# Transposing the gated product of a feed-forward layer: TensorE against VectorE blocks and DMAs

## The chip, the core and the metric

One core of a Trainium2 chip runs the whole program. The metric is the device time of one execution in microseconds (us). The engines are TensorE (PE; its weight loads are shown apart as PEld), VectorE (DVE), ScalarE (ACT), GpSimd (POOL) and SyncE (SP). Each takes its own instructions strictly in its own order.

## What is computed

Two layers of a decoder trunk over 256 positions of width 1024, in float32. Each layer is a feed-forward half-step, a token mixer (gated convolution, sparse attention, cross-attention into 256 memory tokens) and a second feed-forward half-step. The change touches only the feed-forward half-steps, of which there are four:

```python
def swiglu(h, w_in, w_out):
    a, b = jnp.split(h @ w_in, 2, axis=-1)
    return (jax.nn.silu(a) * b) @ w_out

h = rms_norm(x, ffn1_norm_pre[l])
x = x + 0.5 * rms_norm(swiglu(h, ffn1_w_in[l], ffn1_w_out[l]), ffn1_norm_post[l])
```

`w_in` is 1024 x 5632 and `w_out` 2816 x 1024. The product `silu(a) * b` has a position in each row. The second product contracts over its 2816 columns, so TensorE needs it with those columns on the partitions: it has to be transposed.

## The kernel before

**Two streams.** The 256 positions are two streams of 128 rows, t = 0 and t = 1, written as Python generators (`stream`, L1150). A loop (L1159) takes one step of the one, then of the other; stream 0 may be up to three steps ahead. A step is one slice k of a product, six matmuls. A counter `now` counts the steps of both. `later(d, f)` calls f when `now` has gone on by d.

**Products in three matmuls.** Each operand is split in a rounded part and a rest (hi and lo), and `mm3` (L333) runs hi x hi, hi x lo, lo x hi into one PSUM bank (lines L334, L335, L336).

**Weights.** SP loads a unit of 128 x 1024 weights (512 KB) to one of 4 `raw` buffers. ACT writes `whi` (L276, with a gain, or L272), DVE writes `wlo` (L277 or L273), in one of 8 pairs of buffers. Both streams read the same unit, stream 0 first; when stream 1 has read it, its buffer is free. One row of ACT and one of DVE for each unit is thus the beat to which both engines work.

**A feed-forward layer** (`ffn`, L447) runs for j = 0 to 4 a product of 8 steps into two PSUM banks, `pa` and `pb`, then a half-width one (j = 5, 4 steps). After each, `gate` (L452) makes the gated product: ACT a tanh (`th`, L454), DVE two operations (L455 reads `pa`, L456 reads `pb`). When L456 is done the two banks are free. There are six banks of this kind (`psa`): each stream holds two, and two more are what the next product starts on.

**The transposition.** Three steps later `finish_gate` puts four TensorE transposes (L377, two for j = 5) into one of two other PSUM banks (`pst`); ACT copies the bank to `gT` hi (L368), DVE makes `gT` lo (L369). The output product (`output`, L431) then walks k = 0 to 21 over `gT[k // 4]`.

**What else bears on it.** GpSimd computes the small powers of the norms (L389 to L411) and issues a few small DMAs: `rest` (L186) and `stage` (L545 to L549), in layer 0 only, bring gains and constants that TensorE transposes (L188, L551). `begin_layer` starts, at k = 4 of the output product of the first feed-forward layer of each layer, the memory's keys and values, whose transposes (`m`) and products run beside that output product. SBUF tiles of 128 x 1024 come from one pool of 19 (`gtile`). All engines but SP are ordered by a list scheduler with costs of its own, so an instruction need not stand where the code puts it.

Of the kernel before, what the change touches and what calls it, by code (L numbers as in the profile page):

```python
# [21 lines left out]
F32 = mybir.dt.float32  # L22
F32R = mybir.dt.float32r
I32 = mybir.dt.int32
AF = mybir.ActivationFunctionType
OP = mybir.AluOpType
AX = mybir.AxisListType

P = 128
# [22 lines left out]
ABUFS = 6  # L52
LANES = 4
NORM_B, NORM_C = 1, 1
SILU = 3
CMP = 4
ATT_A, ATT_B, ATT_C, ATT_D = 1, 3, 2, 3

# [18 lines left out]


class Nothing:
    """Stands in for engines, pools and tiles while the order of the weight units is found."""  # L80

    def __getattr__(self, name):
        return self
# [11 lines left out]
def view(ap, off, dims):  # L95
    if isinstance(ap, Nothing):
        return ap
    return bass.AP(tensor=ap.tensor, offset=ap.offset + off, ap=[list(ap.ap[0])] + [list(d) for d in dims])


def f32(ap):
    return ap.bitcast(F32)


def trunk_kernel(tc: tile.TileContext, a, out: bass.AP):
    with ExitStack() as ctx:
        def pool(name, bufs, **kw):
            return ctx.enter_context(tc.tile_pool(name=name, bufs=bufs, **kw))

        pools = dict(  # L110
            consts=pool("consts", 1), rawp=pool("rawp", RAWBUFS), wp=pool("wp", WBUFS), gp=pool("gp", GBUFS),
            gbp=pool("gbp", GAINS), tp=pool("tp", TBUFS), sp_pool=pool("sp", 2),
            psa=pool("psa", ABUFS, space=bass.MemoryType.PSUM),
            pst=pool("pst", 8 - ABUFS, space=bass.MemoryType.PSUM))
        nothing = Nothing()
        plan = program(nothing, {k: nothing for k in pools}, nothing, nothing, None)
        with tc.manual_schedule(engines={mybir.EngineType.SP}):
            program(tc.nc, pools, a, out, plan)


def program(nc, pools, a, out, plan):
    dry = plan is None
    consts, rawp, wp, gp, gbp = (pools[k] for k in ("consts", "rawp", "wp", "gp", "gbp"))
    tp, sp_pool, psa, pst = (pools[k] for k in ("tp", "sp_pool", "psa", "pst"))

    class Small:
        @staticmethod
# [12 lines left out]
    def bank(name):  # L140
        return psa.tile([P, 512], F32, name=name, tag="a")

    def tbank():
        return pst.tile([P, 512], F32, name="pt", tag="t")

    def gtile(name, dt=F32):
        return gp.tile([P, 1024], dt, name=name, tag="g")

    def ttile(name, dt=F32):
        return tp.tile([P, 520], dt, name=name, tag="tmp")  # L150

# [1 line left out]
    x = [consts.tile([P, D], F32, name=f"x{t}") for t in range(2)]  # L153
    idle = ttile("idle", F32R)
    nc.vector.memset(f32(idle[:, :512]), 0.0)
# [22 lines left out]
    gT = consts.tile([P, 64], F32, name="gT")  # L178
# [9 lines left out]
        nc.tensor.transpose(pt[:, :48], rest[0:48, 0:P], ident[0:48, 0:48])  # L188
        nc.vector.tensor_copy(gT[:, 16:64], pt[:, :48])

# [1 line left out]
    now = [0]  # L192
    order, found, ready = [], {}, {}
    free = {"raw": RAWBUFS, "w": WBUFS, "g": GAINS}
# [128 lines left out]
    def later(delay, fn):  # L323
        serial[0] += 1
        deferred.append((now[0] + delay, serial[0], fn))
# [40 lines left out]
    def evac_split(hi, lo, ps, scale=None):  # L366
        if scale is None:
            nc.scalar.copy(hi, ps)  # L368
            nc.vector.tensor_sub(lo, ps, f32(hi))  # L369
        else:  # L370
            nc.scalar.activation(hi, ps, AF.Copy, scale=scale)
            nc.vector.scalar_tensor_tensor(lo, ps, scale, f32(hi), op0=OP.mult, op1=OP.subtract)

    def transpose4(src, c0, n=4):
        pt = tbank()
        for j in range(n):
            nc.tensor.transpose(pt[:, j * P:(j + 1) * P], src[:, c0 + j * P:c0 + (j + 1) * P], ident)  # L377
        return pt

# [1 line left out]
    def rstd(halves):  # L381
        ss = sp.tile([P, 2], F32, name="ss2")
        for i in range(2):
            junk = ttile("junk")
            nc.scalar.activation(junk[:, :512], halves[i], AF.Square, accum_out=ss[:, i:i + 1])
        v = sp.tile([P, 1], F32, name="nv")
        nc.vector.scalar_tensor_tensor(v, ss[:, 0:1], D * EPS, ss[:, 1:2], op0=OP.add, op1=OP.add)  # L387
        r = sp.tile([P, 1], F32, name="nr")
        nc.gpsimd.tensor_tensor(r, v, mhalf, op=OP.pow)  # L389
        return r  # L390
# [52 lines left out]
                mm3(y[i], xh, xl, hi[:, sl], lo[:, sl], k == 0, k == count - 1)  # L443
            yield 0

# [1 line left out]
    def ffn(t, l, which):  # L447
        w_in, w_out = f"ffn{which}_w_in", f"ffn{which}_w_out"
        hT, (_, r_half, r2_half, _) = yield from prenorm(x[t], t == 0 and l == 0 and which == 1)
        gT = [None] * 6  # L450

        def gate(j, n, pa, pb):  # L452
            th = ttile("th")
            nc.scalar.activation(th[:, :n], pa[:, :n], AF.Tanh, scale=r_half)  # L454
            nc.vector.scalar_tensor_tensor(th[:, :n], th[:, :n], 1.0, pa[:, :n], op0=OP.add, op1=OP.mult)  # L455
            nc.vector.scalar_tensor_tensor(th[:, :n], th[:, :n], r2_half, pb[:, :n], op0=OP.mult, op1=OP.mult)  # L456

            def finish_gate():
                pt = transpose4(th, 0, n // P)
                gT[j] = gtile("gT", F32R)  # L460
                evac_split(gT[j][:, 0:n], gT[j][:, 512:512 + n], pt[:, :n])

            later(SILU, finish_gate)

        pre = f"ffn{which}_norm_pre"
        for j in range(5):
            pa, pb = yield from product(hT, w_in, l, [(j * 512, 512), (DFF + j * 512, 512)], pre)
            gate(j, 512, pa, pb)
        ps = yield from halves(hT, w_in, l, [(2560, 256), (DFF + 2560, 256)], pre)
        gate(5, 256, ps[:, 0:256], ps[:, 256:512])  # L470
        y = [bank("y0"), bank("y1")]
        def between(k):
            if k == 4 and t == 0 and which == 1:
                begin_layer(l)

        def lhs(k):
            gt, c = gT[k // 4], (k % 4) * P
            return gt[:, c:c + P], gt[:, 512 + c:512 + c + P]

        yield from output(y, w_out, l, 22, lhs, between)  # L480
        yield from postnorm(y, t, (f"ffn{which}_norm_post", l, t), 0.5, which == 2 and l == DEPTH - 1)

# [1 line left out]
    dmask = consts.tile([P, P], F32, name="dmask")  # L484
    cmadd = consts.tile([P, 2, 16], F32, name="cmadd")
    cm01 = consts.tile([P, 2, 16], F32, name="cm01")
# [64 lines left out]
        nc.tensor.transpose(pt[:, :96], stage[0:96, 0:P], ident[0:96, 0:96])  # L551
        nc.vector.tensor_copy(smallT, pt[:, :96])

# [1 line left out]
    shared = {}  # L555

    def begin_layer(l):
# [42 lines left out]
            evac_split(vm[:, 0:512], vm[:, 512:1024], ps[mt], H[mt][1][0])  # L600
            S["vm"].append(vm)

# [1 line left out]
    def rope(src, n, t, write):  # L604
        A = sp.tile([P, n, 2, 8], F32, name=f"ra{n}")
        B = sp.tile([P, n, 2, 8], F32, name=f"rb{n}")
# [442 lines left out]
            yield 0  # L1049
        return ps  # L1050

# [1 line left out]
    pending, lanes, counts = [], [], {}  # L1053

    def add(key, task, front=False):
# [94 lines left out]
    def stream(t):  # L1150
        for l in range(DEPTH):
            yield from ffn(t, l, 1)
            yield from mixer(t, l)
            yield from ffn(t, l, 2)

    streams = [stream(0), stream(1)]
# [59 lines left out]
```

## Time and profile before

| what | value |
|---|---|
| median of 3 runs (lowest to highest) | 1317.28 us (1317.2 to 1317.69) |
| span of the profiled execution | 1314.1 us |
| what the median has beyond that span | 3.2 us |
| TensorE, busy share of the span | 99% |
| VectorE / ScalarE / GpSimd, busy share | 68% / 57% / 6% |
| DMA: hardware queue of SP, share of 16 engines' span | 58% |

The span runs from the first to the last instruction; the profiled execution's own time is its span and about 3 us around it, as the medians are. "Busy" for TensorE is from the modelled start to the modelled end of pipelined matmuls, which overlap: a 128 x 512 matmul is shown with 0.39 us, while the next starts 0.227 us later. Costs on TensorE are therefore read from start to start.

### The profile page before, as it was taken

The numbers are of one execution on the slowest core, as the hardware profiler recorded it, in microseconds if no ns is written. First come the engines' busy times: TensorE is split into PE (matmuls) and PEld (weight loads), VectorE is DVE, ScalarE is ACT, GpSimd is POOL, SyncE is SP. The second block draws the span as 40 slices with busy tenths as digits, with TensorE's granted clock in tenths as the row PEclk, the third lists the DMA queues.
The fourth block names the chain that finished last, engine by engine and source line by source line (L and its number), as shares of the span: only waits on it lengthen the run. The fifth ranks groups of instructions, "written<-read, shape, count | busy, mean of one in ns | idle before, by whom it ended". The sixth has DMA issues, their size and how long they took to land.

```text
span 1314.1 us, 17407 instructions
## 1 busy us (share of the span) xinstructions
PE 1300.3 (99%) x6266; PEld 1078.9 (82%) x6266; DVE 896.6 (68%) x1363; ACT 743.0 (57%) x1195; POOL 76.5 (6%) x184
## 2 busy tenths in 40 slices
PE   9999999999999999999999999999999999999998
PEld 7888888878888888888888888888888888888886
DVE  6666556989887666565575665579898866766643
ACT  6645546886664465454464555568666554645542
POOL 3010101200000010000010001013000000100000
PEclk9999999999999999999999999999999999999999
DMA  8665575764445655655756665657644456566552
GB/s 273 210 192 181 180 220 175 224 214 144 139 134 159 198 187 180 191 192 180 229 168 191 188 209 177 209 167 230 191 144 145 133 159 210 176 188 189 183 190 80
DMA packets 118950, 240.76 MB, mean 183 GB/s; under 512 B 8176, under 2 KB 26768, under 8 KB 118864
## 3 DMA queue, kind: packets, MB, share of 16 engines
q1 hardware_dynamic: 118256, 239.30, 58.0%
q8 instruction: 49, 0.80, 0.2%
q0 software_dynamic: 576, 0.34, 0.1%
q14 instruction: 37, 0.30, 0.1%
q10 hardware_dynamic: 32, 0.01, 0.0%
HBM read 238.57 MB, written 1.05 MB: 182 GB/s over the span
## 4 chain that ended last, share of the span: by engine, by line
PE 90%; DVE 4%; ACT 2%; DMA 2%; issue 1%; POOL 0%; SPq 0%; DVEq 0%; POOLq 0%; ACTq 0%
PE acc L334 19%; PE acc L336 19%; PE acc L335 19%; PE y L336 7%; PE y L335 7%; PE y L334 7%; PE pt L377 3%; PE o L788 2%; PE br L334 2%; PE br L335 2%; PE br L336 2%; DVE wlo L277 1%; DMA raw<-in_ffn_w_in_dram 1%; PE s L745 1%; ACT whi L276 1%
## 5 line engine op out<-in xcount | busy, mean ns | idle before, releaser
L277 DVE SCALAR_TENSOR_TENSOR wlo<-raw,gT,whi 128x512 fp32r<-128x512 f32 (+2 forms) x432 | 397.6, 938 | 208.0 <-ACT whi L276 206.7
L276 ACT ACTIVATE whi<-raw,gT 128x512 fp32r<-128x512 f32 (+2 forms) x432 | 365.9, 874 | 295.3 <-PE acc L336 216.6
L334 PE MATMUL acc<-whi,hThi 128*128 128x512 f32 (+1 forms) x1184 | 468.6, 396 | 1.0 <-ACT hThi L368 1.0
L336 PE MATMUL acc<-whi,hTlo 128*128 128x512 f32 (+1 forms) x1184 | 459.1, 389 | 0.0
L335 PE MATMUL acc<-wlo,hThi 128*128 128x512 f32 (+1 forms) x1184 | 458.6, 388 | 0.1
L336 PEld LDWEIGHTS acc<-whi,hTlo 128*128 128x128 f32 x1184 | 222.1, 188 | 46.9 <-DVE hTlo L369 0.6
L334 PEld LDWEIGHTS acc<-whi,hThi 128*128 128x128 f32 x1184 | 222.5, 188 | 43.1 <-ACT hThi L368 1.8
L335 PEld LDWEIGHTS acc<-wlo,hThi 128*128 128x128 f32 x1184 | 222.7, 188 | 41.8 <-DVE wlo L277 0.8
L273 DVE TENSOR_TENSOR wlo<-raw,whi 128x1024 fp32r<-128x1024 f32 x144 | 176.0, 1224 | 108.2 <-ACT whi L272 106.1
L272 ACT CAST whi<-raw 128x1024 fp32r<-128x1024 f32 x144 | 151.2, 1051 | 130.9 <-PE acc L336 70.6
L334 PE MATMUL y<-whi,gT 128*128 128x512 f32 x352 | 138.1, 392 | 0.0
L336 PE MATMUL y<-whi,gT 128*128 128x512 f32 x352 | 137.4, 390 | 0.0
L335 PE MATMUL y<-wlo,gT 128*128 128x512 f32 x352 | 137.4, 390 | 0.0
L389 POOL TENSOR_TENSOR nr<-nv,mhalf 128x1 f32<-128x1 f32 x28 | 19.9, 712 | 1017.6 <-DVE nv L387 1013.8
L336 PEld LDWEIGHTS y<-whi,gT 128*128 128x128 f32 x352 | 66.1, 188 | 13.8
L335 PEld LDWEIGHTS y<-wlo,gT 128*128 128x128 f32 x352 | 66.1, 188 | 13.3
L334 PEld LDWEIGHTS y<-whi,gT 128*128 128x128 f32 x352 | 66.1, 188 | 13.3
L368 ACT CAST gT<-pt 128x512 fp32r<-128x512 f32 (+1 forms) x48 | 26.1, 543 | 23.3 <-PE pt L377 23.3
L456 DVE SCALAR_TENSOR_TENSOR th<-th,rs,acc 128x512 f32<-128x512 f32 (+1 forms) x48 | 33.7, 703 | 4.5
L454 ACT ACTIVATE th<-acc,rs 128x512 f32<-128x512 f32 (+1 forms) x48 | 31.0, 646 | 7.6 <-PE acc L336 5.8
L455 DVE SCALAR_TENSOR_TENSOR th<-th,acc 128x512 f32<-128x512 f32 (+1 forms) x48 | 30.7, 640 | 6.2 <-ACT th L454 4.4
L369 DVE TENSOR_TENSOR gT<-pt,gT 128x512 fp32r<-128x512 f32 (+1 forms) x48 | 30.9, 643 | 3.9 <-ACT gT L368 3.4
(284 smaller groups left out, 1229.4 us busy)
## 6 DMA issues: line engine op xcount, KB each, us to landing
raw<-in_ffn_w_in_dram SPq DMA_DIRECT2D x160, 512.0 KB, 4.0
raw<-in_w_mix_in_dram SPq DMA_DIRECT2D x96, 512.0 KB, 4.1
raw<-in_ffn_w_out_dram SPq DMA_DIRECT2D x88, 512.0 KB, 3.5
raw<-in_ffn_w_in_dram SPq DMA_DIRECT2D x32, 256.0 KB, 2.9
raw<-in_w_mem_kv_dram SPq DMA_DIRECT2D x16, 512.0 KB, 4.6
raw<-in_w_mix_out_dram SPq DMA_DIRECT2D x16, 512.0 KB, 3.7
gB<-in_ffn_norm_post_dram SPq DMA_DIRECT2D x8, 512.0 KB, 5.6
raw<-in_cmp_k_w_dram SPq DMA_DIRECT2D x8, 512.0 KB, 4.0
```

Source lines behind the costliest of these rows:

```text
L272: nc.scalar.copy(h, v)
L273: nc.vector.tensor_sub(w, v, f32(h))
L276: nc.scalar.activation(h, v, AF.Copy, scale=g)
L277: nc.vector.scalar_tensor_tensor(w, v, g, f32(h), op0=OP.mult, op1=OP.subtract)
L334: nc.tensor.matmul(ps, lhsT=xh, rhs=wh, start=start, stop=False, skip_group_check=skip)
L335: nc.tensor.matmul(ps, lhsT=xh, rhs=wl, start=False, stop=False, skip_group_check=skip)
L336: nc.tensor.matmul(ps, lhsT=xl, rhs=wh, start=False, stop=stop, skip_group_check=skip)
L369: nc.vector.tensor_sub(lo, ps, f32(hi))
L377: nc.tensor.transpose(pt[:, j * P:(j + 1) * P], src[:, c0 + j * P:c0 + (j + 1) * P], ident)
L454: nc.scalar.activation(th[:, :n], pa[:, :n], AF.Tanh, scale=r_half)
L455: nc.vector.scalar_tensor_tensor(th[:, :n], th[:, :n], 1.0, pa[:, :n], op0=OP.add, op1=OP.mult)
L456: nc.vector.scalar_tensor_tensor(th[:, :n], th[:, :n], r2_half, pb[:, :n], op0=OP.mult, op1=OP.mult)
```

## The change

`gate` writes its last result into one half of a 128 x 1024 tile, `wide`. After each odd j the full tile (768 columns for j = 4 and 5 together) goes through `turn_beside`: VectorE transposes it in blocks of 32 x 32 (`blocks`, L388); one step later GpSimd issues four DMAs (`away`, L393), one for each group of 32 partitions, that put the blocks to a scratch in HBM (`there`) so that whole columns lie in a row; two steps after that one DMA (`back`, L400) reads the 512 KB to `moved`; five steps later ACT makes `turnhi` (L406) and DVE `turnlo` (L407) from it. The output product reads those. The TensorE transposes of the gated product, their PSUM banks and the copies L368 and L369 of them are gone. Section comments are blanked as well. Lines of the old kernel stand 2 further down in the new one at L274 to L379, and 32 to 37 further down behind that.

```diff
-SILU = 3
+AWAY, BACK, SPLIT = 1, 3, 8
+DBUFS = 4
...
+            dram=pool("dram", DBUFS, space=bass.MemoryType.DRAM),
...
+    def turn_beside(src, n, put):
+        c, f = n // P, n // 4
+        blocks = gtile("blocks")
+        nc.vector.transpose(blocks[:, :n], view(src, 0, [[32, 4], [P, c], [1, 32]]))
+        there = dram.tile([P, 1024], F32, name="there", tag="d")
+
+        def away():
+            for q in range(4):
+                nc.gpsimd.dma_start(there[:, q * f:(q + 1) * f].rearrange("(p j) f -> j p f", j=32),
+                                    blocks[q * 32:(q + 1) * 32, :n].rearrange("j (p f) -> j p f", p=4))
+
+        moved = []
+
+        def back():
+            moved.append(gtile("moved"))
+            nc.gpsimd.dma_start(moved[0][:, :n], there[:, :n])
+
+        def split():
+            hi, lo = gtile("turnhi", F32R), gtile("turnlo", F32R)
+            dims, r = [[32, c], [f, 4], [1, 32]], "p (c q i) -> p c q i"
+            hv, lv = hi[:, :n].rearrange(r, c=c, q=4), lo[:, :n].rearrange(r, c=c, q=4)
+            nc.scalar.copy(hv, view(moved[0], 0, dims))
+            nc.vector.tensor_sub(lv, view(moved[0], 0, dims), f32(hv))
+            put(hi, lo)
+
+        later(AWAY, away)
+        later(BACK, back)
+        later(SPLIT, split)
...
-        gT = [None] * 6
+        gT, wide = [None] * 3, [None]
...
-            nc.vector.scalar_tensor_tensor(th[:, :n], th[:, :n], r2_half, pb[:, :n], op0=OP.mult, op1=OP.mult)
-
-            def finish_gate():
-                pt = transpose4(th, 0, n // P)
-                gT[j] = gtile("gT", F32R)
-                evac_split(gT[j][:, 0:n], gT[j][:, 512:512 + n], pt[:, :n])
-
-            later(SILU, finish_gate)
+            if j % 2 == 0:
+                wide[0] = gtile("wide")
+            both, c0 = wide[0], j % 2 * 512
+            nc.vector.scalar_tensor_tensor(both[:, c0:c0 + n], th[:, :n], r2_half, pb[:, :n], op0=OP.mult, op1=OP.mult)
+            if j % 2 == 1:
+                turn_beside(both, c0 + n, lambda hi, lo: gT.__setitem__(j // 2, (hi, lo)))
```

The scheduler puts the new instructions among the others. The first place to look at is VectorE in the second feed-forward layer of layer 0, from stream 1's gate of j = 1 to stream 0's gate of j = 2; the other three feed-forward layers have the same rows. Before (the first row is stream 1's L455 of j = 1, the last stream 0's L456 of j = 2; `acc` are the banks `pa` and `pb`):

```order
L455 SCALAR_TENSOR_TENSOR th<-th,acc 128x512
L456 SCALAR_TENSOR_TENSOR th<-th,rs,acc 128x512
L277 SCALAR_TENSOR_TENSOR wlo<-raw,gT,whi 128x1024 x3
L369 TENSOR_TENSOR gT<-pt,gT 128x512
L277 SCALAR_TENSOR_TENSOR wlo<-raw,gT,whi 128x1024 x3
L455 SCALAR_TENSOR_TENSOR th<-th,acc 128x512
L456 SCALAR_TENSOR_TENSOR th<-th,rs,acc 128x512
```

After the change, on VectorE at the same place (L489 and L493 are the gate's two operations, the first `turnlo` is stream 0's, the second stream 1's):

```order
L489 SCALAR_TENSOR_TENSOR th<-th,acc 128x512
L493 SCALAR_TENSOR_TENSOR wide<-th,rs,acc 128x512
L279 SCALAR_TENSOR_TENSOR wlo<-raw,gT,whi 128x1024 x2
L388 STREAM_TRANSPOSE blocks<-wide 128x1024
L279 SCALAR_TENSOR_TENSOR wlo<-raw,gT,whi 128x1024 x2
L407 TENSOR_TENSOR turnlo<-moved,turnhi 128x1024
L279 SCALAR_TENSOR_TENSOR wlo<-raw,gT,whi 128x1024 x2
L489 SCALAR_TENSOR_TENSOR th<-th,acc 128x512
L279 SCALAR_TENSOR_TENSOR wlo<-raw,gT,whi 128x1024 x2
L407 TENSOR_TENSOR turnlo<-moved,turnhi 128x1024
L493 SCALAR_TENSOR_TENSOR wide<-th,rs,acc 128x512
```

Stream 1's `turnlo`, which needs the copy that has come back from HBM, now stands ahead of stream 0's L493 of j = 2, which frees a PSUM bank. ACT has the matching order: eight `whi` lie between stream 1's tanh of j = 1 and stream 1's `turnhi`, four ahead of stream 0's `turnhi` and four behind it.

The second place is GpSimd in layer 0, at the end of the first feed-forward layer. Before (`rs` is the last of a norm, `rest` and `stage` are the small loads named above):

```order
L410 TENSOR_TENSOR rs<-rs 128x1
L186 DMA rest<-in_mix_norm_pre_dram 16x128
L186 DMA rest<-in_ffn_norm_pre_dram 16x128
L186 DMA rest<-in_mem_norm_dram 16x128
L545 DMA stage<-in_cmp_pos_k_dram 16x128
L546 DMA stage<-in_cmp_pos_v_dram 16x128
L547 DMA stage<-in_conv_w_dram 12x128
```

After the change, on GpSimd at the same place (the first row is the last `away` of stream 0, of j = 4 and 5):

```order
L393 DMA there<-blocks 32x4x192 x4
L188 DMA rest<-in_mix_norm_pre_dram 16x128
L188 DMA rest<-in_ffn_norm_pre_dram 16x128
L188 DMA rest<-in_mem_norm_dram 16x128
L577 DMA stage<-in_cmp_pos_k_dram 16x128
L400 DMA moved<-there 128x768
L393 DMA there<-blocks 32x4x192 x4
L578 DMA stage<-in_cmp_pos_v_dram 16x128
L579 DMA stage<-in_conv_w_dram 12x128
L580 DMA stage<-in_cmp_k_b_dram 2x128
L581 DMA stage<-in_cmp_v_b_dram 2x128
L400 DMA moved<-there 128x768
```

The small loads now stand behind the last trips of the gated product, and five more `stage` loads stand behind the last row shown. On TensorE 13 product matmuls lie between the transposes of `rest` and `stage` before the change, and 50 after it.

More of the change, by code (lines that the diff above doesn't have):

```diff
@@ L123, in program @@
     consts, rawp, wp, gp, gbp = (pools[k] for k in ("consts", "rawp", "wp", "gp", "gbp"))
-    tp, sp_pool, psa, pst = (pools[k] for k in ("tp", "sp_pool", "psa", "pst"))
+    tp, sp_pool, psa, pst, dram = (pools[k] for k in ("tp", "sp_pool", "psa", "pst", "dram"))
     class Small:
@@ L476, in lhs @@
         def lhs(k):
-            gt, c = gT[k // 4], (k % 4) * P
-            return gt[:, c:c + P], gt[:, 512 + c:512 + c + P]
+            c = (k % 8) * P
+            return [v[:, c:c + P] for v in gT[k // 8]]
         yield from output(y, w_out, l, 22, lhs, between)
```

## The prediction

> **What bounds the kernel now.** I read the page first: the busy shares, the granted clock, SP's queue and the chain.
>
> ```profile
> span 1314.1 us, 17407 instructions
> PE 1300.3 (99%) x6266; PEld 1078.9 (82%) x6266; DVE 896.6 (68%) x1363; ACT 743.0 (57%) x1195; POOL 76.5 (6%) x184
> ...
> PEclk9999999999999999999999999999999999999999
> ...
> q1 hardware_dynamic: 118256, 239.30, 58.0%
> ...
> PE 90%; DVE 4%; ACT 2%; DMA 2%; issue 1%; POOL 0%; SPq 0%; DVEq 0%; POOLq 0%; ACTq 0%
> ```
>
> TensorE is never out of work, at full clock. Next comes the list of waits, for who waits for whom: first over all engines, then TensorE's own (engine, line, what released it, us in total, times, longest).
>
> ```profile
> ACT whi L276 <- PE acc L336: 216.6, 154, 2.8
> ```
>
> ```profile
> PE pt L377 <- ACT qms L932: 1.6, 2, 0.8
> ...
> PE pt L377 <- DVE th L456: 0.4, 1, 0.4
> ```
>
> ScalarE waits for TensorE to give weight buffers back; TensorE waits almost for nobody. So what is taken off TensorE shortens the run, as long as nothing new makes it wait.
>
> **What the change takes off TensorE.** The timeline of TensorE around four transposes, and around two (start, duration, operation):
>
> ```profile
> 502.84 0.39 PE L336 MATMUL acc<-whi,hTlo 128*128 128x512 f32 x1
> ...
> 503.52 0.39 PE L336 MATMUL acc<-whi,hTlo 128*128 128x512 f32 x1
> 503.75 0.60 PE L377 MATMUL pt<-ident,th 128*128 128x128 f32 x4
> 504.11 0.48 PE L334 MATMUL acc<-whi,hThi 128*128 128x512 f32 x1
> 504.42 0.40 PE L335 MATMUL acc<-wlo,hThi 128*128 128x512 f32 x1
> ```
>
> ```profile
> 606.09 0.39 PE L336 MATMUL y<-whi,gT 128*128 128x512 f32 x1
> 606.32 0.38 PE L377 MATMUL pt<-ident,th 128*128 128x128 f32 x2
> 606.45 0.48 PE L334 MATMUL y<-whi,gT 128*128 128x512 f32 x1
> 606.77 0.40 PE L335 MATMUL y<-wlo,gT 128*128 128x512 f32 x1
> ```
>
> From 502.84 to 503.52 lie three steps: 0.227 us each. From 503.52 to 504.42 (0.90) two steps would take 0.453, so four transposes cost 0.447 us, not the 0.60 shown. From 606.09 to 606.77 (0.68) leaves 0.227 for two. How many there are, and what else goes or comes, I take from the groups by shape (count, busy us, mean ns):
>
> ```profile
> L369 DVE TENSOR_TENSOR gT<-pt,gT 128x512 fp32r<-128x512 f32 x40 | 27.5, 687 | 0.4
> L377 PE MATMUL pt<-ident,th 128*128 128x128 f32 x176 | 27.0, 272 | 0.4 <-DVE th L456 0.4
> L368 ACT CAST gT<-pt 128x512 fp32r<-128x512 f32 x40 | 23.1, 578 | 12.7 <-PE pt L377 12.7
> ```
>
> 176 transposes are 40 groups of four and 8 of two: 40 x 0.447 + 8 x 0.227 = 19.7 us, and 0.4 of waiting for L456 in the list above: **20.1 us off TensorE**. All of it counts, since TensorE is the path.
>
> **What it adds to VectorE and ScalarE.** Nearest rows, SBUF to SBUF:
>
> ```profile
> L273 DVE TENSOR_TENSOR wlo<-raw,whi 128x1024 fp32r<-128x1024 f32 x144 | 176.0, 1224 | 108.2 <-ACT whi L272 106.1
> L272 ACT CAST whi<-raw 128x1024 fp32r<-128x1024 f32 x144 | 151.2, 1051 | 130.9 <-PE acc L336 70.6
> ```
>
> A block transpose of 128 x 1024 stands in no row. Bounds: 0.69 us (L369, half as wide) to 2.4 (twice L273); I take 1.2, L273's. VectorE then loses 40 x 0.69 and 8 narrower ones (together about 31 us) and gains 24 x (1.2 + 1.2), less a quarter for the 8 narrower thirds: about 53. That is 919 of 1297 us: 71%, covered by TensorE. ScalarE gives about 26 and takes 24 x 1.05, less the same: about 23. Nothing on the path.
>
> The Trainium skill (VectorE: DVE Perf Modes, The three transpose paths) gives 311 ns for a 128 x 128 bf16 transpose on VectorE; by it, eight would be an estimated 2.5 us, and the sum would be the same, with the copy below 1.3 us later. No run shows it yet.
>
> **The trip through HBM, and who waits for it.** The output product reads the result tens of us later; it is not the danger. ACT and DVE take `turnhi` and `turnlo` in order, and what stands behind them is. Prices from the DMA issues (count, KB, us to landing) and GpSimd's groups:
>
> ```profile
> raw<-in_ffn_w_out_dram SPq DMA_DIRECT2D x88, 512.0 KB, 3.5
> ...
> gB<-in_mix_norm_post_dram SPq DMA_DIRECT2D x4, 512.0 KB, 6.2
> ...
> w2s<-in_cmp_k_w_dram POOLq DMA_DIRECT2D x2, 64.0 KB, 4.1
> w2s<-in_cmp_v_w_dram POOLq DMA_DIRECT2D x2, 64.0 KB, 4.7
> ...
> stage<-in_cmp_k_b_dram POOLq DMA_DIRECT2D x2, 1.0 KB, 2.3
> ```
>
> ```profile
> L799 POOL DMA_DIRECT2D w2s<-in_cmp_k_w_dram x2 | 1.7, 831 | 0.0
> ...
> L548 POOL DMA_DIRECT2D stage<-in_cmp_k_b_dram x2 | 1.0, 497 | 0.0
> ```
>
> An issue costs GpSimd 0.50 to 0.83 us; I take 0.65. An `away` of 128 KB lands 2.3 to 6.2 us after its issue; I take 4.5, GpSimd's 64 KB rows. A `back` of 512 KB takes 3.5 (SP) to 6.2; I take 5.5, since GpSimd's rows are slower than SP's. From the end of the block transpose: 3 x 0.65 to the last issue, 4.5, then 5.5, and 0.2 between: **12.2 us** (bounds: 1.5 + 2.3 + 3.5 = 7.3 to 2.5 + 6.2 + 6.2 = 14.9). GpSimd has 6% to do and the norms' powers stand behind the last trip, so its 120 issues (24 x 5 x 0.65 = 78 us) stop nobody else, but at the place of `stage`. The traffic grows by 24 x 2 x up to 0.5 MB, 23 MB to 239: SP's 58% become about 64 in all, no limit.
>
> **Place 1, the PSUM banks, four times (once a feed-forward layer).** Stream 0's L493 of j = 2 stands behind stream 1's `turnlo`, and stream 1's product j = 3 starts in the banks that L493 frees. In the clock of before, DVE, ACT and PE:
>
> ```profile
> 522.04 0.75 DVE L456 SCALAR_TENSOR_TENSOR th<-th,rs,acc 128x512 f32<-128x512 f32 x1
> 522.71 1.28 DVE L277 SCALAR_TENSOR_TENSOR wlo<-raw,gT,whi 128x1024 fp32r<-128x1024 f32 x1
> 525.15 1.29 DVE L277 SCALAR_TENSOR_TENSOR wlo<-raw,gT,whi 128x1024 fp32r<-128x1024 f32 x1 [1.16 <-ACT whi L276]
> ...
> 541.95 1.28 DVE L277 SCALAR_TENSOR_TENSOR wlo<-raw,gT,whi 128x1024 fp32r<-128x1024 f32 x1 [1.43 <-ACT whi L276]
> ```
>
> ```profile
> 540.77 1.15 ACT L276 ACTIVATE whi<-raw,gT 128x1024 fp32r<-128x1024 f32 x1 [1.56 <-PE acc L336]
> ```
>
> ```profile
> 541.93 0.60 PE L377 MATMUL pt<-ident,th 128*128 128x128 f32 x4
> ...
> 545.81 0.39 PE L334 MATMUL acc<-whi,hThi 128*128 128x512 f32 x1
> ```
>
> Stream 1's gate ends at 522.8. Two `wlo` are in front of the block transpose, the second ends at 526.4; the transpose at 527.6, the copy lands at 539.8. ACT comes to that `turnhi` after eight `whi`, the last from 540.77 to 541.9 (541.5 without the four transposes at 526.5): the copy is there 1.7 us before. With no late copy, `turnlo` follows the `wlo` that ends at 543.2, to 544.4, and L493 to 545.2; the bank is wanted at 545.81, which without the transposes at 541.93 is 545.4. It just fits: **0 us**, and each us by which the copy lands after 541.5, 13.9 from the transpose's end, is lost on TensorE, four times over. At the upper bound (14.9) that is 4.
>
> **Place 2, `stage` in layer 0, once.** TensorE's transpose of `rest`, and the gate of j = 5 of stream 0:
>
> ```profile
> 143.86 0.26 PE L188 MATMUL pt<-ident,rest 48*128 48x48 f32 x1
> ```
>
> ```profile
> 132.06 0.48 DVE L456 SCALAR_TENSOR_TENSOR th<-th,rs,acc 128x256 f32<-128x256 f32 x1
> ...
> 139.26 0.48 DVE L456 SCALAR_TENSOR_TENSOR th<-th,rs,acc 128x256 f32<-128x256 f32 x1
> ```
>
> Stream 1's gate ends at 139.7; one `wlo` and a transpose of 768 (0.9): 141.9. Four issues start up to 143.9, land by 148.3; `back` goes out, then five `stage` loads (2.5), which land at 153.6. TensorE wants them 50 x 0.227 after `rest`: 143.9 less 0.9 of transposes, plus 11.4, is 154.3. Just ahead; I take 0.5 us, up to 4.
>
> **Place 3, the memory's `m`, twice.** ACT's `turnhi` of j = 4 and 5 stands among the copies of the memory's transposes and the weights for it, where the beat leaves about 1 us; I take 0.4 each, up to 3 each.
>
> **Sum.** Profiled execution: 1314.1 - 20.1 + 0.5 + 0.8 = 1295.3 of span. The median is 3.2 more than the span, which stays: **1298.5 us**, 1.4% faster.
>
> **Rivals.**
>
> *A late copy takes the place of the transposes (slower).* If the trip takes d longer than 13.9 us, TensorE loses 4d at place 1 and about d each at place 2 and twice at place 3: the time is 1317.3 - 20.1 + 7d = 1297.2 + 7d. At d = 2.9 the gain is gone, that is a trip of 16.8, 1.9 beyond my upper bound. Against it: the GpSimd rows above land within 4.7 us. For it: those are single small loads, none through HBM and back, while weights take 58% of the DMA engines. A trip of 19 gives 1297.2 + 7 x 5.1 = 1333 us. Chance 0.07, two hundredths of it within 0.2% of before.
>
> *VectorE holds up GpSimd's issues (slower).* If each issue had to wait for a running `wlo` (1.28 in the rows above), five of them would lengthen the trip by 6.4 to 18.6: 1297.2 + 7 x 4.7 = 1330 us. Against it: L799 took 0.83 us beside a VectorE that is 68% busy. Chance 0.03. The Trainium skill (SBUF — State Buffer, SBUF: two separate sides) has such a rule: while VectorE runs an operation that takes both SBUF ports, GpSimd cannot write a DMA's descriptors. Nothing in the trace so far bears it out, and no row shows whether the block transpose is such an operation.
>
> *A partly late copy, still faster.* A trip of 14 to 16 by the same formula: 1298 to 1312. Bounds allow up to 14.9. Chance 0.14.
>
> *Weights set the pace, so that TensorE's room is not used (same).* For it: 64% of the DMA engines. Against it: 216.6 us of ScalarE's waits are for TensorE. 1317. Chance 0.02.
>
> *The change does not take the transposes off.* The scheduled order has none of them left; no chance is given to it.
>
> **Numbers.** The forecast has 0.74: 1296 to 1302, the low end being 1297.2 with no stall at all and 1 us of small waits that may go. To leave out less than 2 in 10 the range takes in most of the partly late copies: 1295.5 to 1307. About 0.2% (2.6 us) is what a measurement of this kernel can tell from no change. Faster 0.88, same 0.05, slower 0.07.
>
> **What would show it.** Right: TensorE's matmuls fall from 6266 to 6090 and its busy share stays at 99%; TensorE's waits for L493 and for weights stay under 3 us; `turnhi` waits for `moved` seldom; `away` lands in about 4.5 us and `back` in 5.5; STREAM_TRANSPOSE takes about 1.2 us; L583 waits under 1 us. Wrong: hundreds of ns of TensorE before the first matmul of j = 3 of stream 1, ScalarE idle before L406 for several us a time, or a longer GpSimd issue.

## The result

| | before | after |
|---|---|---|
| median (lowest to highest) | 1317.24 us (1315.89 to 1317.69), 4 runs | 1296.5 us (1294.1 to 1298.13), 4 runs |
| ratio after / before, 95% interval | | 0.9843 [0.9829, 0.9857] |
| profiled execution, its span | 1315.89 us, 1314.1 us | 1294.1 us, 1292.4 us |

Faster by 1.6%. From profiled execution to profiled execution it is 21.8 us, from median to median 20.7. The page of the changed kernel: span, engines, granted clock, the two DMA queues, the chain.

```profile
span 1292.4 us, 17239 instructions
...
PE 1278.6 (99%) x6090; PEld 1062.0 (82%) x6090; DVE 915.6 (71%) x1363; ACT 738.2 (57%) x1171; POOL 138.7 (11%) x304
...
PEclk9999999999999999999999999999999999999999
...
q1 hardware_dynamic: 118256, 239.30, 60.0%
q0 software_dynamic: 8128, 23.41, 5.6%
...
PE 92%; DVE 3%; ACT 2%; issue 1%; DMA 1%; POOL 0%; SPq 0%; DVEq 0%; POOLq 0%; ACTq 0%
```

TensorE is 99% busy as before, with 176 matmuls fewer. Its busy time fell by 21.7 us (from 1300.3), and so did the span. GpSimd's queue (q0) now takes 5.6% of the DMA engines. The list of waits, all engines first, then all of TensorE's own (engine, line, what released it, us in total, times, longest):

```profile
ACT whi L278 <- PE acc L338: 186.7, 137, 2.8
...
DVE turnlo L407 <- ACT turnhi L406: 42.8, 17, 7.0
ACT turnhi L406 <- DMA moved<-there: 41.8, 16, 9.3
```

```profile
PE pt L379 <- ACT qms L964: 1.6, 2, 0.8
PE idle L162 <- DVE idle L157: 1.5, 1, 1.5
PE pt L863 <- ACT zc L859: 1.5, 2, 0.8
PE pt L379 <- DVE x L460: 1.2, 5, 0.3
PE acc L336 <- ACT hThi L370: 0.9, 1, 0.9
PE z L853 <- DVE FHL L844: 0.6, 2, 0.3
PE y L338 <- DVE mTlo L374: 0.3, 2, 0.2
```

No line of TensorE's list names L493, `turnhi`, a weight or `stage`. ScalarE does wait for the copies (16 times of 24; a 17th wait, of 8.3 us, stands under `issue` in the list and ends when its copy lands), and VectorE behind it; that comes out of the time in which ScalarE used to wait for TensorE (216.6 us before, 186.7 now). The groups by shape (count, busy us, mean ns, idle before) and the DMA issues (count, KB, median us to landing) give the prices:

```profile
L393 POOL DMA_DIRECT2D there<-blocks x96 | 52.8, 557 | 316.1 <-DVE blocks L388 313.3 <-issue 2.8
...
L388 DVE STREAM_TRANSPOSE blocks<-wide 128x1024 f32<-128x1024 f32 x16 | 19.8, 1237 | 0.0
L407 DVE TENSOR_TENSOR turnlo<-moved,turnhi 128x1024 fp32r<-128x1024 f32 x16 | 19.6, 1224 | 25.7 <-ACT turnhi L406 23.3 <-DMA there<-blocks 2.4
...
L406 ACT CAST turnhi<-moved 128x1024 fp32r<-128x1024 f32 x16 | 16.7, 1046 | 26.3 <-DMA moved<-there 26.3
```

```profile
raw<-in_ffn_w_out_dram SPq DMA_DIRECT2D x88, 512.0 KB, 4.8
there<-blocks POOLq DMA_DIRECT2D x64, 128.0 KB, 4.9
moved<-there POOLq DMA_DIRECT2D x16, 512.0 KB, 5.3
```

From the end of a block transpose to the landing of its copy the 24 trips took 11.1 to 14.6 us; the four at place 1 took 12.5, 12.4, 11.7 and 13.2. Place 1, second feed-forward of layer 0, on VectorE (stream 1's `turnlo`, then stream 0's L493 of j = 2) and on TensorE (the last row is the matmul that wants the bank):

```profile
535.62 1.22 DVE L407 TENSOR_TENSOR turnlo<-moved,turnhi 128x1024 fp32r<-128x1024 f32 x1
536.76 0.74 DVE L493 SCALAR_TENSOR_TENSOR wide<-th,rs,acc 128x512 f32<-128x512 f32 x1
```

```profile
537.57 0.39 PE L338 MATMUL acc<-whi,hTlo 128*128 128x512 f32 x1
537.80 0.39 PE L336 MATMUL acc<-whi,hThi 128*128 128x512 f32 x1
```

The bank is free at 537.50 and wanted at 537.80: 0.3 us to spare, and the same 0.3 in each of the four layers.

### The profile page after: what moved, and what is told of

The parts are those of the page before. It is cut to its first block, busy times and chain, and to the rows that moved or that the text cites. A ratio compares the mean times of both kernels' runs of the same rounds, so it can differ in the third digit from the quotient of the medians.

```text
span 1292.4 us, 17239 instructions
## 1 busy us (share of the span) xinstructions
PE 1278.6 (99%) x6090; PEld 1062.0 (82%) x6090; DVE 915.6 (71%) x1363; ACT 738.2 (57%) x1171; POOL 138.7 (11%) x304
## 4 chain that ended last, share of the span: by engine, by line
PE 92%; DVE 3%; ACT 2%; issue 1%; DMA 1%; POOL 0%; SPq 0%; DVEq 0%; POOLq 0%; ACTq 0%
PE acc L336 20%; PE acc L338 19%; PE acc L337 19%; PE y L338 7%; PE y L337 7%; PE y L336 7%; PE pt L379 2%; PE o L820 2%; PE br L336 2%; PE br L338 2%; PE br L337 2%; PE s L777 1%; DVE wlo L279 1%; PE pt L801 1%; ACT whi L278 1%
## 5 line engine op out<-in xcount | busy, mean ns | idle before, releaser
L278 ACT ACTIVATE whi<-raw,gT 128x512 fp32r<-128x512 f32 (+2 forms) x432 | 365.3, 873 | 268.0 <-PE acc L338 186.7
L274 ACT CAST whi<-raw 128x1024 fp32r<-128x1024 f32 x144 | 150.9, 1051 | 105.6 <-PE acc L338 57.2
L338 PE MATMUL y<-whi,turnlo 128*128 128x512 f32 x352 | 137.5, 391 | 0.0
L337 PE MATMUL y<-wlo,turnhi 128*128 128x512 f32 x352 | 137.4, 390 | 0.0
L336 PE MATMUL y<-whi,turnhi 128*128 128x512 f32 x352 | 136.3, 390 | 0.0
L393 POOL DMA_DIRECT2D there<-blocks x96 | 52.8, 557 | 316.1 <-DVE blocks L388 313.3
L338 PEld LDWEIGHTS y<-whi,turnlo 128*128 128x128 f32 x352 | 66.1, 188 | 13.6
L337 PEld LDWEIGHTS y<-wlo,turnhi 128*128 128x128 f32 x352 | 66.1, 188 | 13.5
L336 PEld LDWEIGHTS y<-whi,turnhi 128*128 128x128 f32 x352 | 66.0, 188 | 13.5
L407 DVE TENSOR_TENSOR turnlo<-moved,turnhi 128x1024 fp32r<-128x1024 f32 (+1 forms) x24 | 27.2, 1135 | 45.2 <-ACT turnhi L406 42.8
L406 ACT CAST turnhi<-moved 128x1024 fp32r<-128x1024 f32 (+1 forms) x24 | 23.4, 976 | 52.2 <-DMA moved<-there 41.8
L489 DVE SCALAR_TENSOR_TENSOR th<-th,acc 128x512 f32<-128x512 f32 (+1 forms) x48 | 30.6, 638 | 7.7 <-ACT th L488 7.7
```

The costliest lines, as they stand in the source:

```text
L274: nc.scalar.copy(h, v)
L278: nc.scalar.activation(h, v, AF.Copy, scale=g)
L336: nc.tensor.matmul(ps, lhsT=xh, rhs=wh, start=start, stop=False, skip_group_check=skip)
L337: nc.tensor.matmul(ps, lhsT=xh, rhs=wl, start=False, stop=False, skip_group_check=skip)
L338: nc.tensor.matmul(ps, lhsT=xl, rhs=wh, start=False, stop=stop, skip_group_check=skip)
L393: nc.gpsimd.dma_start(there[:, q * f:(q + 1) * f].rearrange("(p j) f -> j p f", j=32), blocks[q * 32:(q + 1) * 32, :n].rearrange("j (p f) ...
```

## The experiments

The theory: TensorE is the bound, the gain is what a group of transposes takes from it, and the trip costs nothing because nothing that TensorE needs soon stands behind the wait for it. The rivals: the gain is in the PSUM banks and copies that went; the trip costs something that the gain hides; VectorE, GpSimd or the DMAs are near a limit.

| run | median, us | ratio to before, 95% interval |
|---|---|---|
| e1, transposes kept beside the change | 1321.63 | 1.0035 [1.0024, 1.0047] |
| e2, no transposition at all | 1294.76 | 0.9833 [0.9818, 0.9848] |
| h1, the change in layer 1 alone | 1309.46 | 0.9943 [0.993, 0.9955] |
| t3, turnlo three times | 1302.9 | 0.9904 [0.9886, 0.9921] |
| d2, trips put off by two copies | 1307.02 | 0.9922 [0.9909, 0.9936] |
| d4, by four copies | 1319.75 | 1.0016 [1.0, 1.0031] |
| d4s, four copies, split later | 1316.16 | 0.9995 [0.9973, 1.0016] |
| f2, four copies, second feed-forwards alone | 1307.22 | 0.9929 [0.9916, 0.9943] |
| e3, a second trip | 1412.87 | 1.074 [1.0715, 1.0766] |
| e4, a second trip, split later | 1391.37 | 1.0566 [1.0541, 1.0592] |
| e6, the memory's tiles turned as well | 1304.7 | 0.9895 [0.9878, 0.9912] |
| e9, the same with later products | 1294.81 | 0.9826 [0.9811, 0.9841] |

### Where the gain comes from: e1, e2, h1

e1 puts TensorE's transposes back, beside everything new:

```diff
             nc.vector.scalar_tensor_tensor(both[:, c0:c0 + n], th[:, :n], r2_half, pb[:, :n], op0=OP.mult, op1=OP.mult)
+            later(3, lambda: transpose4(both, c0, n // P))
             ...
```

> The changed kernel, with TensorE's 176 transposes put back beside it: three units after each gated product TensorE transposes it into a PSUM bank that nobody reads; the block transposes, the trip through HBM and the split stay. Theory (the gain is TensorE's own time for the transposes, 40 groups of four at 0.447 us and 8 of two at 0.227 us = 19.7 us): all of it comes back, about 1296.5 + 20 = 1316.5 us, 6266 matmuls, TensorE 99% busy. Rival (the gain comes from the copies out of PSUM that ACT and DVE no longer make, or from the banks that they held): those stay away here, so at most a few us come back, 1297 to 1301 us.

1321.63 us, 25 more than the changed kernel. The page and the one new line of TensorE's waits:

```profile
PE 1301.8 (99%) x6266; PEld 1079.0 (82%) x6266; DVE 915.7 (69%) x1363; ACT 738.2 (56%) x1171; POOL 143.7 (11%) x304
```

```profile
PE pt L379 <- DVE wide L493: 3.8, 5, 1.5
```

All of the gain went, and 3.8 us more in which the transposes waited for L493, a wait that this way of putting them back makes. The run's 25 us over the changed kernel are thus more than the gain, and some 1.6 us of its longer span are not put down to anything. ScalarE and VectorE still do without the copies out of PSUM, so those were not the gain.

e2 is the kernel before without any transposition:

```diff
-                pt = transpose4(th, 0, n // P)
                 ...
-                evac_split(gT[j][:, 0:n], gT[j][:, 512:512 + n], pt[:, :n])
+                evac_split(gT[j][:, 0:n], gT[j][:, 512:512 + n], th[:, :n])
```

> The kernel before with the transposition left out: ACT and DVE split the gated product as it lies in SBUF, no transposes on TensorE, no block transposes, no trip (the result is then not the reference's). It is the floor for any way of moving the transposes off TensorE. Theory (the trip of the changed kernel is hidden wholly): as the changed kernel, 1295 to 1298 us. Rival (late copies cost the changed kernel something at the PSUM banks, at the layer's start or at the memory's tiles): lower than the changed kernel by that cost, 1290 to 1294 us.

```profile
span 1293.8 us, 17037 instructions
...
PE 1279.4 (99%) x6090; PEld 1062.3 (82%) x6090; DVE 895.7 (69%) x1363; ACT 747.0 (58%) x1195; POOL 76.4 (6%) x184
```

1294.76 us: its interval and the changed kernel's overlap, and its profiled span is 1.4 us longer than the changed kernel's. The trip leaves nothing to be won back that these runs can tell. (It fell 0.2 us below the range in which the theory had it.) The PSUM banks come back with the transposes in e1 and go with them in e2, so these two runs do not part banks from transposes; but in the kernel before no line of TensorE's waits names a copy out of these banks to `gT`.

h1 makes the change in layer 1 alone (`if l == 0:` the old `finish_gate`, else the new path).

> The change made in layer 1 alone: layer 0's gated products go through TensorE's transposes and the copies out of PSUM as in the kernel before, layer 1's through the blocks and the scratch. Theory (the gain is TensorE's time for each group of transposes that goes, and the trip is hidden): half of it, 20 groups of four and 4 of two, by the spans 21.7 / 2 = 10.9 us below before, 1306 us. Rival (part of the gain or of a hidden loss sits in layer 0, where place 2 is): more than 2 us away from that, under 1304 or over 1308 us.

1309.46 us, by the letter the rival's side. The trace shows where it comes from. The last matmul starts at 1298.3 us, in the kernel before at 1307.8, in the changed one at 1286.0; half way is 1296.9. Of the 1.4 us beyond, 1.2 are one wait of TensorE's:

```profile
PE pt L379 <- DVE th L496: 1.2, 1, 1.2
```

The rest of the difference lies behind the last matmul: from there to the end it takes 9.2 us here and 6.3 in the other two. The output's last DMA lands 2.1 us behind VectorE's last instruction in all three; what ends later is one of GpSimd's closing instructions, a DRAIN (L1256) that takes 7.1 us here and 2.8 (L1244) in the changed kernel. Why it took longer is open. On TensorE the half is half.

### VectorE's room and place 1: t3

```diff
+            nc.vector.tensor_sub(lv, view(moved[0], 0, dims), f32(hv))
+            nc.vector.tensor_sub(lv, view(moved[0], 0, dims), f32(hv))
             nc.vector.tensor_sub(lv, view(moved[0], 0, dims), f32(hv))
```

> The changed kernel with VectorE's half of the split (turnlo, 1.22 us) done three times over, the same result each time: 24 x 2 x 1.2 less a quarter for the eight narrower ones, about 54 us more on VectorE, as much as the change added, 915.6 to about 970 us or 75%. No DMA, no trip and nothing on TensorE changes. Theory (TensorE is the bound and VectorE has room, so that work on VectorE costs nothing by itself): 1295 to 1300 us, with TensorE's waits under 3 us more than in the changed kernel. Rival (VectorE is near its limit in the feed-forward products, where the bank at place 1 came free 0.3 us before TensorE wanted it): 2 x 1.2 us at place 1 four times and more at the gates, 1305 us or over.

1302.9 us, between the two. VectorE rose to 74% of the span (961.9 us), and two lines of TensorE's waits are new and large:

```profile
PE pt L190 <- DMA rest<-in_mem_norm_dram: 2.2, 1, 2.2
PE acc L336 <- DVE wide L495: 1.9, 4, 0.6
```

The second is place 1, four times, once a feed-forward layer. In the timeline at the same point as above, VectorE, then TensorE (L495 is the old L493):

```profile
543.05 1.22 DVE L407 TENSOR_TENSOR turnlo<-moved,turnhi 128x1024 fp32r<-128x1024 f32 x1
544.19 0.74 DVE L495 SCALAR_TENSOR_TENSOR wide<-th,rs,acc 128x512 f32<-128x512 f32 x1
```

```profile
544.02 0.39 PE L338 MATMUL acc<-whi,hTlo 128*128 128x512 f32 x1
544.98 0.50 PE L336 MATMUL acc<-whi,hThi 128*128 128x512 f32 x1 [0.57 <-DVE wide L495]
```

L495 ends at 544.93 and the matmul starts at 544.98. By matmul starts the four waits put TensorE back by 0.4 to 0.8 us each. So place 1 is as the prediction drew it: the bank, the instruction in front of it, and no slack but the 0.3 us. The other cost is place 2, about 4.5 us in the first output product of layer 0: the 2.2 us of wait for `rest`, and behind it 3.4 us (144.2 to 147.6) in which the granted clock is 0.50, which costs an estimated 1.7 more. The 46 us that VectorE did more cost 6.4 us, by the waits mainly where an instruction or a small load had been on time by tenths.

### How late a copy may come: d2, d4, d4s, f2

GpSimd copies the blocks onto themselves before it issues `away`, twice (d2) or four times (d4); each copy of 128 x 1024 took 1.32 us (d2) and 1.39 (d4).

```diff
         def away():
+            for _ in range(4):
+                nc.gpsimd.tensor_copy(blocks[:, :n], blocks[:, :n])
             ...
```

> The changed kernel with each trip put off: GpSimd copies the transposed blocks onto themselves twice (128 x 1024 float32, about 1.1 us each by GpSimd's memset of that size) before it issues the four DMAs. In the changed kernel the copies at place 1 land 11.7 to 13.2 us after the block transpose, and by the prediction's working TensorE waits from 13.9 us on. Stream 1's trip stands behind stream 0's on GpSimd (stream 0's second DMA is issued only 8.2 us after its transpose, about when stream 1's starts), so stream 1 gets the delay twice, about 4.4 us: copies at 17, 3 us late. Theory (each us behind 13.9 costs TensorE a us at place 1, four times, and up to three times more at the two other places): 1308 to 1317 us. Rival (the engines' buffers and the other banks give more room than that): 1295 to 1299 us.

> The same with four copies on GpSimd, about 4.4 us, 8.8 us for stream 1: copies at 21.3 us, 7.4 late. Theory: 4 x 7.4 = 30 us at place 1, up to 52 with the others: 1326 to 1348 us. Rival (more room): 1295 to 1305 us.

1307.02 and 1319.75 us: 1 and 6 us under the theory's ranges, and not at the place that it named. At place 1 the copies landed at 16.0 to 17.5 us (d2) and at 17.7 to 20.1 (d4) behind the block transpose, and TensorE's waits of d2 show nothing there:

```profile
PE y L336 <- ACT whi L274: 3.9, 2, 2.3
PE pt L190 <- DMA stage<-in_cmp_pos_v_dram: 2.8, 1, 2.8
```

The scheduler knows of the copies and had put VectorE in another order. At place 1 in d2 (L491 is the old L489):

```
L491 SCALAR_TENSOR_TENSOR th<-th,acc 128x512
L279 SCALAR_TENSOR_TENSOR wlo<-raw,gT,whi 128x1024 x2
L491 SCALAR_TENSOR_TENSOR th<-th,acc 128x512
L279 SCALAR_TENSOR_TENSOR wlo<-raw,gT,whi 128x1024
L409 TENSOR_TENSOR turnlo<-moved,turnhi 128x1024
L495 SCALAR_TENSOR_TENSOR wide<-th,rs,acc 128x512 x2
```

Both streams' L491 of j = 2 now stand ahead of `turnlo`, each frees the bank of its `pa`, and stream 1's j = 3 starts in those two. What was lost lies in the output product of the first feed-forward: comparing the start of each matmul with the changed kernel's (the same count in both, in places in another order), d2 loses 7.0 of its 10.8 us there in layer 0 and 3.0 in layer 1, d4 some 11 and 9 of 25.8. Of d2's 7.0, place 2 has about 4.5: the wait of 2.8 and a half clock behind it. Elsewhere there ScalarE's `whi` for the output weights stands behind a `turnhi` that waits. ScalarE, then TensorE, in d4:

```profile
162.27 0.83 ACT L408 CAST turnhi<-moved 128x768 fp32r<-128x768 f32 x1 [6.05 <-issue]
163.00 1.04 ACT L274 CAST whi<-raw 128x1024 fp32r<-128x1024 f32 x1
```

```profile
164.10 1.22 PE L336 MATMUL y<-whi,turnhi 128*128 128x512 f32 x2 [4.75 <-ACT whi L274]
...
165.54 0.63 PE L337 MATMUL y<-wlo,turnhi 128*128 128x512 f32 x1
165.97 0.63 PE L338 MATMUL y<-whi,turnlo 128*128 128x512 f32 x1
```

That copy landed at 162.1, 20.6 us behind its block transpose. It is the prediction's place 3, with another price: weights, several us at a time.

The last two rows show a second part of the price. The matmuls start 0.43 us apart in place of 0.227: from 163.2 to 170.0 the granted clock is 0.50. Neither the kernel before nor the changed one has such a stretch ahead of its last matmul. The delayed kernels have stretches of 3.4 us or a multiple of it at or behind most of their waits of over 2 us. Outside of the waits themselves they cost an estimated 4.9 us in d4 and 1.7 in each of d2, t3 and f2 (half of the time in them in which TensorE did not wait). So a wait of a few us costs TensorE more than its own length. What makes the clock fall is not followed here.

d4s names the split 14 units behind the gate instead of 8 (`AWAY, BACK, SPLIT = 1, 3, 14`).

> Four copies on GpSimd as well, with the split named 14 units behind the gate instead of 8. VectorE's order then has stream 0's L493 of j = 2 behind stream 0's turnlo, whose copy lands 8 us sooner, and no longer behind stream 1's. Theory (what costs is the place of the wait in VectorE's queue, not the length of the trip): place 1 is free again, and what is left is at most the two other places, up to 3 x 7.4 us: 1297 to 1318 us. Rival (the trip's length itself costs, as through tiles that are held longer): as with the split at 8 units, 1326 to 1348 us.

1316.16 us, at the top of the theory's range and not told apart from d4 by much. Place 1 had cost d4 only 2.3 us, in the last layer, so freeing it could not give much; in layer 0 the delay of `rest` on GpSimd (6.9 us of TensorE's wait) took the place of the waits at place 3, and the waits for `whi` of the output weights are still 8.5 us (12.1 in d4). That the length of the trip costs by itself is not shown either.

> The delay of four GpSimd copies (1.27 us each as measured) in the second feed-forward of each layer alone; the first ones have no delay. With the delay everywhere TensorE lost 25.8 us of span, and by the matmuls' start times some 20 of it in the output products of the two first feed-forwards, where stage and the memory's tiles are. Theory (a late copy costs TensorE only where something that it needs soon stands behind the wait, which is at stage and among the memory's copies): at most 1 to 6 us over the changed kernel, 1297 to 1303 us. Rival (the lateness costs in every feed-forward, at the PSUM banks): half of the 25.8, over 1307 us.

1307.22 us, above the theory's range and just over the rival's 1307: the memory's place is not the only one. TensorE lost 11.2 us, 4.6 of them in the last output product (the last feed-forward's j = 4 and 5; 2.7 of wait, the rest mostly half clock) and 2.1 at place 1 of that layer, where the copy landed at 20.3:

```profile
PE y L336 <- DVE wide L495: 2.7, 1, 2.7
...
PE acc L336 <- DVE th L491: 1.8, 1, 1.8
```

The other 4.5 us are spread, 1.1 of them ahead of the first trip. So a trip some 6 us longer shows at places where one of the two engines has something for TensorE behind the wait. What stays open is how much of the 10.7 us is lateness and how much is the scheduler's new order, which came with the delay.

### A second trip: e3, e4

```diff
+            moved.append(gtile("moved"))
             nc.gpsimd.dma_start(moved[0][:, :n], there[:, :n])
+            again = dram.tile([P, 1024], F32, name="again", tag="d")
+            nc.gpsimd.dma_start(again[:, :n], moved[0][:, :n])
+            nc.gpsimd.dma_start(moved[1][:, :n], again[:, :n])
             ...
```

> The changed kernel with a second trip: what came back goes to another scratch and comes back once more, two more DMAs of 512 KB behind the first. In the changed kernel ScalarE's split starts 12 to 16 us after the end of the block transpose; the second trip adds some 11 us (two landings of about 5.3 us and two issues of 0.56 us). Theory (VectorE's half of the split stands ahead of the other stream's L493, whose PSUM bank TensorE needs by 13.9 us after the block transpose, four times): copies at about 25 us are 11 us late, and TensorE waits for four of them, 44 us, up to seven with the other places, 1341 to 1374 us. Rival (there is far more room than reckoned, since VectorE catches up): 1296 to 1305 us.

> The same second trip, with the split moved from 8 to 18 units behind the gated product (10 units of 1.36 us = 13.6 us later), so that the other stream's L493 no longer stands behind it there. Theory (only the place of the split in the engines' queues makes a late copy cost TensorE's time; the traffic itself, about 23 MB more, does not): 1295 to 1300 us. Rival (the DMA traffic or GpSimd's issues cost by themselves, through weights that land later): over 1305 us, with waits of ACT or TensorE for raw weights.

1412.87 and 1391.37 us. e3 lost 119 us of span, far over the theory's upper end, and moving the split (18 units) won back 21.5 us of the 116 between the medians. GpSimd's waits in e4:

```profile
POOL moved L401 <- DMA there<-blocks: 130.4, 23, 9.1
POOL again L403 <- DMA moved<-there: 114.0, 24, 6.9
POOL moved L404 <- DMA again<-moved: 106.2, 21, 7.0
```

GpSimd stands in front of each DMA until the one before it has landed, so the two streams' trips hardly overlap: stream 1's `away` started up to 17.6 us behind its block transpose in e4 and 16.4 in e3 (0.3 to 1.6 in the changed kernel), with `rest` and `stage` behind it. By matmul starts place 1 cost e3 4.5 to 6.8 us each time, not 11, the two output products beside the memory about 30 us each, and the two others 19 and 11. The page of e3 shows the clock, too:

```profile
PEclk9999879999999999998999998899999999999999
```

By the estimate used for d4, its half clock costs 35 us, and its waits are 78 us more than the changed kernel's. In e4 place 1 costs nothing any more, and 95 us of loss stay, so the place of the split there was not most of it. By the letter it is the rival's: it came out over 1305 us, and ScalarE's waits for the raw weights of the feed-forward layers rose from 7.7 us in the changed kernel to 54.0:

```profile
ACT whi L278 <- DMA raw<-in_ffn_w_in_dram: 29.2, 22, 3.2
...
ACT whi L274 <- DMA raw<-in_ffn_w_out_dram: 24.8, 18, 5.9
```

Those loads land only a little later, though (medians 5.0 and 5.5 us, 4.8 in the changed kernel), and TensorE's largest waits are for `turnhi` and `whi`. One queue in order for both streams fits that; no run parts it from the traffic.

### Taking off more: e6, e9

The memory's tiles `m` go the same way, 32 transposes fewer; in e9 both trips start first and the products come 18 units behind.

```diff
-            H.append((yield from prenorm(m)))
-        yield 6
+            turned.append([])
+            turn_beside(m, 1024, turned[mt].extend)
+            H.append((yield from prenorm(m, beside=True)))
+        yield 18
         ...
```

> The changed kernel with the memory's tiles (m, 128 x 1024, two in each layer) turned the same way: block transpose, trip, split, instead of 32 more transposes on TensorE, 8 groups of four. Theory (a transpose costs what it takes from TensorE, start to start, and a hidden trip nothing): 8 x 0.447 = 3.6 us less, 1293 us. Rival (four more trips beside the output product, on the same GpSimd queue as those of j = 4 and 5, come late for the memory's products): 1296 to 1305 us.

> The memory's tiles turned beside TensorE again, but both trips start before the memory's task waits, and its products come 18 units later instead of 9 and 6 in a row; two more scratch buffers. In the first try TensorE waited 6.9 us for the memory's turnhi and 2.1 for rest. Theory (only the wait that stands in front of the memory's products ate the gain of 3.6 us): 1292.5 to 1295 us. Rival (the longer queue on GpSimd delays rest, stage and the copies of j = 4 and 5 as well): 1297 to 1305 us.

e6: 1304.7 us, in the rival's range. TensorE's waits in e6, then in e9:

```profile
PE acc L336 <- ACT turnhi L406: 6.9, 2, 5.6
PE pt L190 <- DMA rest<-in_mem_norm_dram: 2.1, 1, 2.1
```

```profile
PE pt L190 <- DMA rest<-in_mem_norm_dram: 2.1, 1, 2.1
...
PE y L336 <- ACT whi L274: 1.6, 1, 1.6
```

e9: 1294.81 us, within the theory's range, at its upper end. The wait for `turnhi` is gone and the one for `rest` stays; one of 1.6 us for `whi` is new. With an estimated 1.7 us of half clock behind the wait for `rest` these eat the 3.6 us; against the changed kernel (0.9826 against 0.9843, the intervals overlap) no gain can be told.

## Why the prediction was right, point by point

- **TensorE is the bound**: right. 99% busy at full clock on both sides of the change. In the experiments work added elsewhere showed through waits of TensorE's and the half clock behind them.
- **20.1 us off TensorE**: right, 1.6 short. The span fell by 21.7, and e1 brought all of it back. The term took the two matmuls behind each group into account; the ten steps after those are up to 8 ns longer each as well. Summed over all starts of 128x512 matmuls that do not follow a transpose directly, that excess fell by about 1.9 us: 0.04 us for each of the 48 groups.
- **VectorE 919 us, ScalarE less 3**: 915.6, and 738.2 from 743.0. The block transpose took 1.24 us where 1.2 was taken. By the Trainium skill (VectorE: DVE Perf Modes, The three transpose paths: 311 ns for 128 x 128 in bf16) it would have been an estimated 2.5. The measurement decides: this form, 1024 float32 columns, costs as much as a subtraction of that size (L407, 1.22).
- **The trip, 12.2 us (7.3 to 14.9)**: 11.1 to 14.6, at place 1 12.5, 12.4, 11.7, 13.2. Its parts: issue 0.56 us where 0.65 was taken, `away` 4.9 for 4.5, `back` 5.3 for 5.5.
- **Place 1, 0 us with 0.2 to spare**: right, 0.3 to spare, and t3 shows the wait there as soon as it is used up. That each us by which a copy is late is lost four times over was worked out for an unchanged order, and no run tests it there; the scheduler's order for a longer trip moves an L489 ahead and gives some 4 us more (of d4's four copies, 3.8 to 6.2 us late, one alone cost TensorE a wait there, of 1.9).
- **Place 2, 0.5 us**: nothing in the changed kernel; the term was 0.5 too large. It is as near as was said, `stage` landing 0.7 us before TensorE takes it. But `rest`, for which the working set no wait, landed only 0.5 us ahead, and it is at the transpose of `rest` (L190) that TensorE waits 2 to 3 us in t3, d2, e6 and e9 (in d2 the list names `stage` as what released it; `rest` had landed 0.3 us before).
- **Place 3, 0.8 us**: nothing. The bound was too low, though: with trips of 20 us an output product loses 9 to 11 us (d4, an estimated 2 to 3 of it by the half clock), as weights stand behind the wait.
- **3.2 us around the span**: wrong. That was the median's distance to a profiled execution that was itself 1.4 us under the median; around the span there are 1.8.
- **`turnhi` waits for `moved` seldom**: wrong, at least 16 of 24 times, 41.8 us. The working looked at the place where ScalarE comes last; elsewhere the scheduler's order has `turnhi` nearer to its copy. It costs TensorE nothing here, as ScalarE waits for TensorE anyway.
- **Sum**: 1298.5 forecast. The profiled execution came to 1294.1, 4.4 less: places 2 and 3 cost nothing (1.3), the groups cost 1.6 more, and 1.4 around the span were counted twice. The median, 1296.5, lies 2.4 above that execution, so the forecast is nearer to it than its terms are, by luck of which execution was profiled.
- **The rivals**: a late copy did not come. (The chances given to the rivals one by one add up to 0.04 for same and 0.08 for slower, where the prediction states 0.05 and 0.07.) Where a late copy was made, the formula 1297.2 + 7d was too steep: d2's copies, 2.1 to 3.6 us late, give 1312 to 1322 us by it and took 1307, d4's (3.8 to 6.2) 1324 to 1341 and took 1320, since place 1 gave way. VectorE did not hold up GpSimd's issues: 557 ns a piece in the changed kernel, and the same 557 in t3 with VectorE at 74%. The rule of the Trainium skill (SBUF — State Buffer, SBUF: two separate sides) thus leaves no mark on these issue times; whether the landing times hold some of it was not tested. Weights did not set the pace: ScalarE still waits 186.7 us for TensorE at L278 alone.

## What to carry to other kernels

Where TensorE is busy throughout and others wait for it, a transposition is worth what it takes between the starts of its neighbours, and a way through VectorE and HBM of some 13 us is free, as long as what TensorE needs within those 13 us does not stand behind the waiting instruction on its engine's queue. Look for that instruction by name and measure its slack: here it was 0.3 us at one place, and for four tiles more the same trade gave no gain that could be told. Count the clock as well: where TensorE did wait, for 2 us and more, it mostly ran at half clock for 3.4 us or longer at the wait. And when a delay is put in to test such slack under a scheduler, compare the orders first, since the scheduler answers it.

## What the runs showed of the hardware that was not expected

- The granted clock of TensorE, 1.00 otherwise up to the last matmul, fell to 0.50 for 3.4 us or a multiple of it at or behind most of its waits of over 2 us; a 128x512 matmul then started 0.43 us behind the one before, in place of 0.227.
- Behind a group of four transposes not only the step from the first matmul to the second is longer (315 ns in place of 227), but the ten steps after it as well, by up to 8 ns each.
- Weights of 512 KB on SP's queue took 4.8 us to land where they took 3.5 before (`in_ffn_w_out`), although GpSimd's queue holds only 5.6% of the DMA engines; ScalarE waited 3.9 us in all for them, TensorE not at all.
- In the changed kernel GpSimd's DMAs of 128 KB landed in 3.2 to 6.8 us and those of 512 KB in 3.6 to 7.8, one form each; the 24 trips, the smaller ones among them, have a spread of 3.5 us.
